# A streamed two-layer trunk on one core: state products interleaved with projections, earlier adaLN pieces, and a third fixed expert in the second unit

## The chip, the cores and the metric

The kernel runs on one core of one Trainium2 chip. The metric is the device time of one execution in microseconds (us), the median over several runs. A core has a matrix engine (TensorE, PE in the profile, with its weight loads as PEld), a vector engine (DVE), a scalar engine (ACT), GpSimd (POOL) and SyncE (SP), which here does little else than issue the transfers of the weights. Each engine works through its own queue of instructions in order and waits for others by semaphores.

## The reference

The input is one sequence of 256 tokens of 1024 numbers. It passes through two layers, each a mixer and a mixture of experts, with weights in float32. Cut to what matters:

```python
cond = jax.nn.silu(c)
for i in range(2):
    sh1, sc1, g1, sh2, sc2, g2 = jnp.split(cond @ ada_w[i] + ada_b[i], 6, axis=-1)
    h = modulate(rmsnorm(x, norm_mix_g[i]), sh1, sc1)
    mix = gla_mixer(...) if i == 0 else lru_mixer(...)
    x = x + g1[:, None] * mix
    h = modulate(rmsnorm(x, norm_ffn_g[i]), sh2, sc2)
    x = x + g2[:, None] * grouped_moe(h, router_w, router_bias, w_gate[i], w_up[i], w_down[i])
return rmsnorm(x, final_norm_g)

def grouped_moe(...):      # per token: sigmoid scores, the best of 4 groups, the best 2 of its 4 experts
    for e in range(16):
        he = silu(t @ w_gate[e]) * (t @ w_up[e])          # 1024 -> 512
        out = out + combine[:, e:e + 1] * (he @ w_down[e])
```

`gla_mixer` is gated linear attention in chunks of 64 tokens: projections q, k, v and g, a state per chunk and head (k transposed times v, decayed), the output q times the state, normalised and multiplied by silu(g). Each token goes to two experts, so 512 pairs of token and expert are spread over 16 experts as the router decides. Which expert gets how many is data, and the inputs are drawn once from a fixed seed.

## The kernel before

**The stream of weights.** All large weights pass through one ring of 17 tiles of 1 MB (`SLOTS`). `plan` writes down the order of the pieces as a text: `a20` is the two pieces of adaLN column block 2, half 0 (`A` those of layer 1), `i4` two pieces of the mixer's input projection, `I3` and `J3` its first and second half alone, `o` the four of the output projection, `u0` the pieces of MoE unit 0. `Stream.get` hands out the next tile and calls `ahead`, which has SP issue transfers up to `look` pieces further on. A piece can be issued when its ring tile is free and when it is `known`: a piece of an expert that is chosen by rank is known only when `route_order` has written the list of ranks, `order[l]`.

**adaLN on DVE.** `fill` takes one job of a list: it gets two `a` pieces and lets DVE multiply them into a row (`scalar_tensor_tensor`, L317). `settle` later has TensorE sum and turn these rows.

**Layer 0's mixer (`gla`).** `half_proj` forms k and v, then q is formed (L613), then the products of the states (L629) for both tiles of 128 tokens, which DVE copies and scans out of the PSUM banks (L637), then the projection of g by `g_part` through `tok_proj` (L529), and `o_part`, `gated`, `turn`. `out_route` does the output projection (L473) together with the router.

**The MoE.** Tokens are gathered by expert into units of 128 rows, four slots of 32. `UNITS` lists them: `("s", 0, 2)` is the fixed expert 0 with 2 slots, `("r", 1, 3)` the expert that stands at rank 1 among those that are not fixed, sorted by their count of tokens, with 3 slots. `NS` is the number of fixed experts. `route_order` sorts, `route_end` works out where each expert's rows stand and compares each count with the expert's slots times 32 (`ce`). If one is greater, `fl` is 1. Each unit uses 12 MB of weights or more: two pieces of each of gate, up and down for each expert in it. `up_proj` (L1030) runs for gate and up, `down_proj` (L1041) and `scatter` (L1060, L1061) follow.

**`overflow`.** Ahead of unit 5 (`len(UNITS) - 2`) every engine reads the flag and branches (L1067). Only if it is set, a loop runs over all 16 experts (L1079 on): for each it loads the six pieces one after the other into the tile `h` (L1082), multiplies all 256 tokens with them, and adds the result for the tokens whose rank in their expert lies beyond the slots.

The pieces of code on which these words rest:

```python
V.tensor_tensor(ovf, cnt, ce, op=OP.is_gt)           # route_end
V.tensor_reduce(fl, ovf, axis=AX.X, op=OP.max)
...
with tc.If(flag > 0):                                # overflow, L1067
    ...
    with tc.For_i(0, NE, 1) as e:                    # L1079
        def load(name, n, j, q):
            t = h.rearrange("p m n -> p (m n)")
            nc.sync.dma_start(t, I[name][l][ds(e, 1), q * n:(q + 1) * n, :]...)   # L1082
```

Of the kernel before, what the change touches and what calls it, by code (L numbers as in the profile page):

```python
# [10 lines left out]
OP = mybir.AluOpType  # L11
# [3 lines left out]
P = 128  # L15
D = 1024
S = 256
NM = S // P
# [8 lines left out]

UNITS = [
    [("s", 0, 2), ("s", 1, 2)],
    [("r", 0, 3), ("r", 8, 1)],  # L30
    [("r", 1, 3), ("r", 9, 1)],
    [("r", 2, 2), ("r", 3, 2)],
    [("r", 4, 2), ("r", 5, 2)],
    [("r", 6, 2), ("r", 7, 2)],
    [("r", 10, 1), ("r", 11, 1), ("r", 12, 1), ("r", 13, 1)],
]
NS = 2
ND = NE - NS
SLOTS = 17
HALVES = [slice(0, 512), slice(512, 1024)]  # L40
# [35 lines left out]
def trunk(ctx, tc, I, out):  # L76
# [10 lines left out]
    def bank():  # L87
        return pp.tile([P, 512], F32, name="ps")
# [134 lines left out]
    late = []  # L223
# [6 lines left out]
    def moe_piece(l, name, kind, i, s, last):  # L230
        src = I[name][l]
        n, j = (512, 4) if name != "moe_w_down" else (256, 2)
        last = last and name == "moe_w_down"

        def f(t):
            if kind == "s":
                assert not last
                a = src[i, s * n:(s + 1) * n, :].rearrange("(p j) n -> p (j n)", j=j)
            else:
                if (l, i) not in regs:  # L240
                    with tc.issue_after(mark["load"]):
                        regs[l, i] = nc.sync.value_load(order[l][0:1, i:i + 1], min_val=NS, max_val=NE - 1)
                a = src[ds(regs[l, i], 1)]
                if last:

                    late.append((t, a))
                    part(t, a, s)
                    if len(late) == 2 * len(UNITS[-1]):
                        for q in range(2, len(TAIL)):
                            for t, a in late[len(UNITS[-1]):]:  # L250
                                part(t, a, q)
                        late.clear()
                    return
                a = a[:, s * n:(s + 1) * n, :].rearrange("o (p j) n -> (o p) (j n)", j=j)
            b = nc.sync.dma_start(t, a)  # L255
            mark["load"] = b.ins
        f.known = lambda: kind == "s" or order[l] is not None
        return f

    def moe_pieces(l, unit):  # L260
        return [moe_piece(l, name, kind, i, s, unit is UNITS[-1]) for name in ("moe_w_gate", "moe_w_up", "moe_w_down")
                for s in range(2) for kind, i, n in unit]

# [2 lines left out]
    def plan(l, text):  # L266

        for n in text.split():
# [13 lines left out]
            else:  # L282
                stream.add("u", *moe_pieces(l, UNITS[int(n[1])]))

    plan(0, "a10 a00 I2 a11 I3 a01 I1 J2 J3 J1 i0 a20 a21 i4 a40 a41 i5 a30 a31 a50 a51 o A10 A11 A00 A01 "
            "u0 u1 u2 u3 u4 u5 u6")
    plan(1, "i2 i3 a20 r i0 a21 a40 i1 a41 a30 a31 o a50 a51 u0 u1 u2 u3 u4 u5 u6")

# [171 lines left out]
    def out_route(l, yT, gate, gs, rest=None, last=None):  # L460

        w = [stream.get("o").rearrange("p (j n) -> p j n", j=2) for _ in range(4)]
        stream.look = SLOTS - 2
        h, hT = new_h()
        R = route_begin()

        def part(m, hf, between={}):
            sl = slice(hf * 512, (hf + 1) * 512)
            ps = bank()
            for k in range(8):  # L470
                if k in between:
                    between[k]()
                T.matmul(ps, yT[:, k, m * P:(m + 1) * P], w[k // 2][:, k % 2, sl], start=k == 0, stop=k == 7)  # L473
            tmp = s2("tmp")
            V.tensor_mul(tmp, ps, gate[:, sl])
            b = V.tensor_add(x[:, m, sl], x[:, m, sl], tmp)
            mark["x"] = b.ins

        def first():
            turn_h(x, hT, 0, halves=[1])  # L480
            stats_of[0] = stats(0)
            scaled(h, 0, stats_of[0])

        late = len(jobs) > 2
        stats_of = [None, None]
        with tc.manual_schedule(engines={T.engine}):
            part(0, 0)
            part(0, 1, {3: lambda: turn_h(x, hT, 0, halves=[0])})
            if rest:
                rest()  # L490
            router(R, gs)
            part(1, 0, {2: lambda: settle(2), 4: first, 6: lambda: router_shift(R, gs[1], 0), 7: lambda: logits(R, hT, 0)})
            router_shift(R, gs[1], 1)
            scores(R, 0, stats_of[0])
            choose(R, 0)
            fill(2)
            part(1, 1, {3: lambda: turn_h(x, hT, 1, halves=[0]), 5: lambda: logits(R, hT, 1, halves=[0]),
                        7: lambda: route_count(R, 0)})
            stream.ahead(stream.at + SLOTS - 1)
            r = stats(1)  # L500
            if late:
                accs = mid("acc")
                fill_now(accs[:, 0:512])
            else:
                settle(1)
            turn_h(x, hT, 1, halves=[1])
            xg, oh = gather_begin(R)
            gather_tile(R, h, oh, 0, 0, [0])
            logits(R, hT, 1, halves=[1])
            scores(R, 1, r)  # L510
            scaled(h, 1, r)
            gather_tile(R, h, oh, 0, 0, [1, 2, 3])
            choose(R, 1)
            gather_tile(R, h, oh, 0, 1)
            route_count(R, 1)
            if late:
                fill_now(accs[:, 512:1024])
            else:
                settle(1)
            if last:  # L520
                last()
            gather_end(l, R, h, xg, gs)
        R["xg"] = xg
        return h, hT, R
# [7 lines left out]
    def get2():  # L532
        return [stream.get("i").rearrange("p (j n) -> p j n", j=4) for _ in range(2)]


    def gla(gs):
# [40 lines left out]
            T.matmul(ps[32 * q:32 * q + 32, 0:S], wa[:, k, :], hT[:, k, :], start=k < 4, stop=k >= 4)  # L577
        V.tensor_scalar(alr, ps[:, 0:S], e16, None, op0=OP.add)
        half_proj(0, 1)
        for m in range(NM):  # L580
            A.copy(v[:, m, 0:512], pst[0][m])

# [5 lines left out]
        for m in range(NM):  # L588
            A.activation(ed[:, m], ed[:, m], AF.Ln, bias=1.0)
            V.scalar_tensor_tensor(la[:, m], psz[m], 0.0, ed[:, m], op0=OP.min, op1=OP.subtract)  # L590
        half_proj(1, 1)
        for m in range(NM):
            A.copy(v[:, m, 512:1024], pst[1][m])
        half_proj(2, 1)
        psg = bank()
        for m in range(NM):
            ps = bank()
# [12 lines left out]
        for hd in range(4):  # L610
# [1 line left out]
            for k in range(8):  # L612
                T.matmul(ps[:, 0:S], w[k // 4][:, k % 4, hd * P:(hd + 1) * P], hT[:, k, :], start=k == 0, stop=k == 7)  # L613
            A.activation(qT[:, hd], ps[:, 0:S], AF.Copy, scale=128.0 ** -0.5)
        fill(2)
        k0.extend(lru_consts())


        Sb = [big("S").rearrange("p (c n) -> p c n", c=2) for _ in range(2)]
        St = [Sb[c // 2][:, c % 2].rearrange("p (h n) -> p h n", h=4) for c in range(4)]  # L620

        for m in range(NM):
            for h2 in range(2):
                pair = [bank(), bank()]
                for hh in range(2):
                    hd = 2 * h2 + hh
                    for c in range(2):
                        rows_of = slice(64 * c, 64 * c + 64)
                        T.matmul(pair[c][:, hh * 256:(hh + 1) * 256], kd[rows_of, m, hd * P:(hd + 1) * P],  # L629
                                 v[rows_of, m, hd * 256:(hd + 1) * 256], start=True, stop=True)  # L630
                for c in range(2):
                    k = 2 * m + c
                    for hh in range(2):
                        hd = 2 * h2 + hh
                        src = pair[c][:, hh * 256:(hh + 1) * 256]
                        if k == 0:
                            V.tensor_copy(St[k][:, hd], src)  # L637
                        else:
                            V.scalar_tensor_tensor(St[k][:, hd], St[k - 1][:, hd], gam[:, hd * 4 + k:hd * 4 + k + 1],
                                                   src, op0=OP.mult, op1=OP.add)  # L640
        sg = big("sg").rearrange("p (m n) -> p m n", m=2)

        def g_part(hf, m, w):
# [26 lines left out]
        def turn(m, hf):  # L670
# [4 lines left out]
            for b in range(2):  # L675
# [4 lines left out]
                else:  # L680
                    V.tensor_scalar(dst, src, ngT[:, b:b + 1], None, op0=OP.mult)

        w = get2()
        for m in range(NM):
            g_part(0, m, w)
        fill(2)
        os = [o_part(m) for m in range(NM)]
        for m in range(NM):
            gated(m, 0, *os[m])
        settle(2)  # L690
        w = get2()
        g_part(1, 0, w)
        gated(0, 1, *os[0])
# [2 lines left out]
            turn(m, 0)  # L696
        g_part(1, 1, w)
        gated(1, 1, *os[1])
        fill(4)
        settle(2)  # L700
        turn(0, 1)
        return oT[0], lambda: turn(1, 1)

# [289 lines left out]
    def moe(l, h, hT, R, gs, g2, done=None):  # L993
# [18 lines left out]
        def groups(unit):  # L1012
# [7 lines left out]
                at += n  # L1020
            return res

        def up_proj(unit, xg, t0):
            ps = bank()
            for s in range(2):
                w = [stream.get("u").rearrange("p (j n) -> p j n", j=4) for _ in unit]
                for j in range(4):
                    k = 4 * s + j
                    for i, p0, n in groups(unit):
                        T.matmul(ps[p0:p0 + n], xg[:, k, t0 + p0:t0 + p0 + n], w[i][:, j, :], start=k == 0, stop=k == 7)  # L1030
            return ps
# [217 lines left out]
```

## Time and profile before

| | us |
|---|---|
| median of three runs | 759.18 |
| the three runs | 758.07, 759.18, 760.01 |
| profiled execution | 757.96 |
| its span | 756.2 |
| TensorE busy | 699.6 (93%) |
| DVE busy | 340.4 (45%) |
| ACT busy | 131.4 (17%) |

The span is the time from the first to the last recorded instruction; 1.8 us of the execution lie around it. A share of busy time is a mean over stages with different limits, so a stage has to be looked at by itself. The granted clock is 1.00 where TensorE runs at its higher level and 0.50 where it runs at its lower one. Transfers moved 286.27 MB, a mean of 379 GB/s over the span. In the timeline a group of instructions has its start, its length, and in square brackets the idle time ahead of it with what ended it.

### The profile page before, as it was taken

How to read it: one execution, taken by the hardware profiler on the slowest of the kernel's cores; microseconds unless marked ns; L12 is line 12 of the kernel's file. 1: busy time of each engine (PE TensorE's matmuls, PEld its weight loads, DVE VectorE, ACT ScalarE, POOL GpSimd, SP SyncE). 2: the span in 40 equal slices, each digit the busy share in tenths (PEclk: the TensorE clock that was granted, in tenths of full speed). 3: DMA queues.
4: the chain of work that ended last, by engine and by line, in shares of the span. 5: the costliest groups of instructions: out<-in, count | busy, mean ns of one | idle time of the engine just before them, and what ended most of it. 6: DMA issues, size and time to landing. Idle time of an engine off the chain costs nothing. (4 is left out here: it accounts for less than half of the span.)

```text
span 756.2 us, 9538 instructions
## 1 busy us (share of the span) xinstructions
PE 699.6 (93%) x3559; PEld 342.8 (45%) x3559; DVE 340.4 (45%) x780; ACT 131.4 (17%) x257; POOL 27.4 (4%) x69
## 2 busy tenths in 40 slices
PE   4899899999999999999887999998999999999874
PEld 3345745454633533533226888655433433433212
DVE  3626983897413223231023589996523143140214
ACT  5006112122200000000013166123210010010002
POOL 5000001000000000000000014000000000000000
PEclk9999999999999999999999999999999999999998
DMA  9999999779999999999999999991999999999994
GB/s 304 384 386 387 386 396 386 269 318 384 423 370 422 421 421 420 423 409 422 411 363 379 381 367 350 406 377 59 423 421 419 419 421 421 421 420 410 422 373 150
DMA packets 80445, 286.27 MB, mean 379 GB/s; under 512 B 5991, under 2 KB 16280, under 8 KB 57866
## 3 DMA queue, kind: packets, MB, share of 16 engines
q1 hardware_dynamic: 78752, 284.71, 96.0%
q10 hardware_dynamic: 1258, 0.66, 0.3%
q8 instruction: 30, 0.49, 0.3%
q0 software_dynamic: 384, 0.23, 0.1%
q14 instruction: 21, 0.17, 0.1%
HBM read 284.54 MB, written 1.05 MB: 378 GB/s over the span
## 5 line engine op out<-in xcount | busy, mean ns | idle before, releaser
L1030 PE MATMUL ps<-w 128*32 128x512 f32 (+1 forms) x1280 | 204.1, 593 | 9.6 <-DMA w<-in_moe_w_up_dram 7.4
L1030 PEld LDWEIGHTS ps<-w 128*32 128x32 f32 (+1 forms) x1280 | 61.8, 121 | 148.7 <-issue 121.7
L1041 PE MATMUL ps<-w,s 128*32 128x512 f32 (+1 forms) x512 | 85.0, 594 | 2.7 <-ACT s L1160 2.7
L1147 DVE TENSOR_TENSOR s<-s,ps 128x512 f32<-128x512 f32 x14 | 9.6, 688 | 149.6 <-PE ps L1030 149.6
L1061 DVE TENSOR_TENSOR x<-x,ps 128x512 f32<-128x512 f32 (+1 forms) x60 | 39.1, 652 | 59.7 <-PE ps L1060 59.7
L317 DVE SCALAR_TENSOR_TENSOR acc<-w,cond,acc 128x512 f32<-128x512 f32 x84 | 64.8, 794 | 1.1
L473 PE MATMUL ps<-w 128*128 128x512 f32 x128 | 59.3, 599 | 0.0
L1060 PE MATMUL ps<-mid,s 128*128 128x512 f32 (+1 forms) x120 | 55.1, 581 | 2.9 <-DVE mid L1168 2.6
L740 PE MATMUL ps<-hT,w 128*128 128x256 f32 x256 | 55.7, 379 | 0.0
L1041 PEld LDWEIGHTS ps<-w,s 128*32 128x32 f32 (+1 forms) x512 | 25.6, 123 | 58.3 <-issue 50.9
L740 PEld LDWEIGHTS ps<-hT,w 128*128 128x128 f32 x256 | 48.7, 191 | 6.7 <-ACT hT L423 0.2
L1179 DVE TENSOR_TENSOR mid<-ps,gate 128x512 f32<-128x512 f32 x24 | 16.6, 692 | 64.7 <-PE ps L1041 64.7
L561 PE MATMUL ps<-w,hT 128*128 128x512 f32 x96 | 42.5, 596 | 1.8 <-DVE hT L425 1.0
L904 PE MATMUL ps<-onehot,h 128*128 128x256 f32 x192 | 42.4, 379 | 0.0
L317 DVE SCALAR_TENSOR_TENSOR gate<-w,cond,gate 128x512 f32<-128x512 f32 x56 | 40.9, 748 | 0.9
L1146 ACT ACTIVATE s<-ps 128x512 f32<-128x512 f32 x14 | 8.4, 597 | 183.6 <-PE ps L1030 183.6
L904 PEld LDWEIGHTS ps<-onehot,h 128*128 128x128 f32 x192 | 36.4, 190 | 7.0 <-issue 2.4
L1060 PEld LDWEIGHTS ps<-mid,s 128*128 128x128 f32 x120 | 20.5, 190 | 30.8 <-issue 20.1
L1160 ACT COPY s<-ps 128x512 f32<-128x512 f32 x14 | 8.2, 586 | 147.2 <-PE ps L1158 147.2
L529 PE MATMUL ps<-w,hT 128*128 128x512 f32 x64 | 29.6, 619 | 3.7 <-DVE w L637 3.7
L473 PEld LDWEIGHTS ps<-w 128*128 128x128 f32 x128 | 22.8, 191 | 20.7 <-issue 18.9
L561 PEld LDWEIGHTS ps<-w,hT 128*128 128x128 f32 x96 | 17.8, 190 | 23.9 <-issue 21.0
(261 smaller groups left out, 602.5 us busy)
## 6 DMA issues: line engine op xcount, KB each, us to landing
w<-in_moe_w_gate_dram SPq DMA_DIRECT2D x64, 1024.0 KB, 11.2
w<-in_moe_w_up_dram SPq DMA_DIRECT2D x64, 1024.0 KB, 15.7
w<-in_moe_w_down_dram SPq DMA_DIRECT2D x56, 1024.0 KB, 17.8
w<-in_ada_w_dram SPq DMA_DIRECT2D x48, 1024.0 KB, 13.5
w<-in_gla_w_in_dram SPq DMA_DIRECT2D x12, 1024.0 KB, 14.6
w<-in_moe_w_down_dram SPq DMA_DIRECT2D x16, 512.0 KB, 9.5
w<-in_lru_w_in_dram SPq DMA_DIRECT2D x8, 1024.0 KB, 12.5
w<-in_gla_w_out_dram SPq DMA_DIRECT2D x4, 1024.0 KB, 12.5
```

What stands on the lines that cost most here:

```text
L317: V.scalar_tensor_tensor(acc, w, cond[:, k:k + 1], acc, op0=OP.mult, op1=OP.add)
L473: T.matmul(ps, yT[:, k, m * P:(m + 1) * P], w[k // 2][:, k % 2, sl], start=k == 0, stop=k == 7)
L529: T.matmul(ps, hT[:, k, m * P:(m + 1) * P], w[k // 4][:, k % 4, :], start=k == 0, stop=k == 7)
L561: T.matmul(pst[i][m], hT[:, 4 * b + j, m * P:(m + 1) * P], w[:, j], start=b == 0 and j == 0, stop=b == 1 and j == 3)
L740: T.matmul(ps[:, 0:S], w[k // 4][:, k % 4, ct * P:(ct + 1) * P], hT[:, k, :], start=k == 0, stop=k == 7)
L904: T.matmul(ps[j // 2][:, j % 2 * 2 * P:(j % 2 + 1) * 2 * P], hv[:, b, j, :], oh, start=m == 0 and j % 2 == 0, stop=m == 1 and j % 2 == 1, ...
L1030: T.matmul(ps[p0:p0 + n], xg[:, k, t0 + p0:t0 + p0 + n], w[i][:, j, :], start=k == 0, stop=k == 7)
L1041: T.matmul(ps[hf][p0:p0 + n], aT[:, k, p0:p0 + n], w[i][:, j, hf * 512:(hf + 1) * 512], start=k == 0, stop=k == 3)
L1060: T.matmul(ps, wt[:, m * P:(m + 1) * P], y[:, sl], start=True, stop=True)
L1061: V.tensor_add(x[:, m, sl], x[:, m, sl], ps)
L1147: V.tensor_mul(act, act, pu)
L1179: V.tensor_mul(y[:, sl], py[hf], g2[:, sl])
```

## The change

Three things are altered.

First, the units of the MoE. `NS` is 3: expert 2 is fixed too and shares unit 1 with rank 1, which now has two slots instead of three. Rank 0 and rank 8 move to unit 2, and the last unit holds ranks 9 to 12. Unit 1's pieces come in another order, gate and up of expert 2 first, and `up_proj` takes its pieces by a list `held` to match.

Second, the order of layer 0's pieces: `a20`, `a21`, `a40`, `a41`, `a30` and others stand among the input projections, and `A10 A11` ahead of `o`. The calls of `fill` and `settle` follow: one `fill` behind each of three `half_proj`, and none within `out_route` of layer 0 (`late` is true there).

Third, `states(m)` is a function, called ahead of `g_part(0, m)` for each tile of tokens, where all states stood before all of the projection.

```diff
 UNITS = [
     [("s", 0, 2), ("s", 1, 2)],
+    [("s", 2, 2), ("r", 1, 2)],
     [("r", 0, 3), ("r", 8, 1)],
-    [("r", 1, 3), ("r", 9, 1)],
...
-    [("r", 10, 1), ("r", 11, 1), ("r", 12, 1), ("r", 13, 1)],
+    [("r", 9, 1), ("r", 10, 1), ("r", 11, 1), ("r", 12, 1)],
 ]
-NS = 2
+NS = 3
...
     def moe_pieces(l, unit):
+        if unit is UNITS[1]:
+
+            return [moe_piece(l, name, kind, i, s, False) for kind, i, n in unit for name in ("moe_w_gate", "moe_w_up")
+                    for s in range(2)] + [moe_piece(l, "moe_w_down", kind, i, s, False) for s in range(2) for kind, i, n in unit]
...
-    plan(0, "a10 a00 I2 a11 I3 a01 I1 J2 J3 J1 i0 a20 a21 i4 a40 a41 i5 a30 a31 a50 a51 o A10 A11 A00 A01 "
+    plan(0, "a10 a00 I2 a11 I3 a01 I1 J2 a20 J3 a21 J1 a40 i0 a41 a30 i4 a31 a50 a51 i5 A10 A11 o A00 A01 "
             "u0 u1 u2 u3 u4 u5 u6")
...
-        late = len(jobs) > 2
+        late = rest is not None
...
-            fill(2)
+            if not late:
+                fill(2)
...
         half_proj(0, 1)
+        fill()
...
         half_proj(1, 1)
+        fill()
...
         half_proj(2, 1)
+        fill()
...
-        fill(2)
+        fill()
+        settle(3)
+        fill()
         k0.extend(lru_consts())
...
         w = get2()
         for m in range(NM):
+            states(m)
             g_part(0, m, w)
-        fill(2)
+        settle(1)
+        with tc.issue_after(mark["states"]):
+            fill(3)
...
-        settle(2)
...
-        fill(4)
         settle(2)
+        fill(2)
         turn(0, 1)
...
+        held = []
+
         def up_proj(unit, xg, t0):
             ps = bank()
+            if unit is UNITS[1] and not held:
+                look, stream.look = stream.look, stream.look - 4
+                held.extend(stream.get("u") for _ in range(4))
+                stream.look = look
             for s in range(2):
-                w = [stream.get("u").rearrange("p (j n) -> p j n", j=4) for _ in unit]
+                w = [(held.pop(0) if held and i == 0 else stream.get("u")).rearrange("p (j n) -> p j n", j=4)
+                     for i in range(len(unit))]
```

On SP, in layer 0 from the output projection's pieces to the first piece of an expert that is chosen by rank (`TENSOR_LOAD r_ordi` reads the list of ranks), before:

```order
L211 DMA w<-in_gla_w_out_dram 128x2x1024 x4
L196 DMA w<-in_ada_w_dram 128x4x512 x8
L255 DMA w<-in_moe_w_gate_dram 128x2048 x4
L255 DMA w<-in_moe_w_up_dram 128x2048 x4
L255 DMA w<-in_moe_w_down_dram 128x2048 x4
L242 TENSOR_LOAD r_ordi
```

and now:

```order
L196 DMA w<-in_ada_w_dram 128x4x512 x4
L211 DMA w<-in_gla_w_out_dram 128x2x1024 x4
L196 DMA w<-in_ada_w_dram 128x4x512 x4
L255 DMA w<-in_moe_w_gate_dram 128x2048 x4
L255 DMA w<-in_moe_w_up_dram 128x2048 x4
L255 DMA w<-in_moe_w_down_dram 128x2048 x4
L255 DMA w<-in_moe_w_gate_dram 128x2048 x2
L255 DMA w<-in_moe_w_up_dram 128x2048 x2
L242 TENSOR_LOAD r_ordi
```

Four adaLN pieces moved ahead of the output projection, and four pieces of expert 2 (gate and up) now stand ahead of the list of ranks.

On TensorE, in layer 0 from the q projection (L613, now L621) to the second half of the g projection (L529, now L534); a product of the order is two passes in the trace. The states are L629 (now L681), `o_part` L655 (now L645). Before:

```order
L613 MATMUL ps<-hT,w 128x256 x32
L707 MATMUL ps<-ident,s_158 128x64
L629 MATMUL ps<-w,h 128x256 x16
L529 MATMUL ps<-w,hT 128x512 x16
L655 MATMUL ps<-w,mid 64x256 x16
```

and now:

```order
L621 MATMUL ps<-hT,w 128x256 x32
L353 MATMUL ps<-gate,one 128x512 x2
L357 MATMUL ps<-ident,acc 128x128 x4
L721 MATMUL ps<-ident,s_160 128x64
L681 MATMUL ps<-w,h 128x256 x8
L534 MATMUL ps<-w,hT 128x512 x8
L681 MATMUL ps<-w,h 128x256 x8
L534 MATMUL ps<-w,hT 128x512 x8
L357 MATMUL ps<-ident,acc 128x128 x4
L645 MATMUL ps<-w,mid 64x256 x16
```

The sixteen products of the states are split in two lots of eight with eight of the projection between them, and sums of adaLN rows stand ahead of them and behind.

## Rows read from the trace of the kernel before

**Rows 1.** The page, busy time, share of the span, instructions:
```profile
PE 699.6 (93%) x3559; PEld 342.8 (45%) x3559; DVE 340.4 (45%) x780; ACT 131.4 (17%) x257; POOL 27.4 (4%) x69
```

**Rows 2.** Windows around layer 1's routing; columns in the first line:
```profile
core 0: us, PE busy (x) PEld busy (x) DVE busy (x) ACT busy (x) POOL busy (x), PEclk, DMA share, GB/s
...
510.00:520.00 10.00, 8.74 (x41) 5.36 (x41) 5.79 (x29) 2.82 (x7) 0.55 (x1) 1.00 0.27 107
520.00:530.00 10.00, 8.62 (x51) 5.57 (x52) 7.29 (x38) 4.15 (x9) 0.00 (x0) 1.00 0.14 39
530.00:540.00 10.00, 10.00 (x50) 3.37 (x48) 5.98 (x30) 1.78 (x2) 0.00 (x0) 1.00 1.00 423
```

**Rows 3.** Timeline of TensorE: start, length, line, operation, [idle ahead <- releaser]:
```profile
73.37 14.00 PE L613 MATMUL ps<-hT,w 128*128 128x256 f32 x64
...
94.81 15.51 PE L529 MATMUL ps<-w,hT 128*128 128x512 f32 x32 [3.72 <-DVE w L637]
...
131.68 8.75 PE L473 MATMUL ps<-w 128*128 128x512 f32 x20
...
332.23 9.23 PE L1030 MATMUL ps<-w 128*64 128x512 f32 x42 [1.33 <-DVEq L1067]
...
481.04 9.61 PE L473 MATMUL ps<-w 128*128 128x512 f32 x22
```

**Rows 4.** Windows around the pause at 91 us, layer 0:
```profile
91.00:94.40 3.40, 0.09 (x2) 0.00 (x0) 2.95 (x19) 0.00 (x0) 0.00 (x0) 1.00 1.05 387
94.50:97.80 3.30, 2.99 (x4) 1.44 (x5) 3.30 (x10) 0.00 (x0) 0.00 (x0) 0.50 1.05 387
97.90:101.30 3.40, 3.40 (x9) 1.48 (x8) 3.37 (x8) 0.00 (x0) 0.00 (x0) 1.00 1.05 387
```

**Rows 5.** The instructions of one line, asked for the loop's load:
```profile
nothing on L1082; most used: ['L1030', 'L1041', 'L255', 'L740', 'L1052', 'L904', 'L473', 'L1060', 'L561', 'L317', 'L353', 'L766', 'L338', 'L529', 'L613', 'L830', 'L922', 'L1158', 'L433', 'L227', 'L196', 'L242', 'L1061', 'L818', 'L629']
```

**Rows 6.** The same view of the branch's line; durations in ns, minimum, median, maximum:
```profile
L1067 PEldq COMPARE_BRANCH  x2: 318/335/352, 328.9 to 674.0; - x2
```

**Rows 7.** DMA issues at 466, 160, 336 and 556 us; KB, us to landing:
```profile
w<-in_lru_w_out_dram SPq DMA_DIRECT2D x1, 1024.0 KB, 4.8
...
w<-in_moe_w_up_dram SPq DMA_DIRECT2D x1, 1024.0 KB, 4.9
...
w<-in_moe_w_gate_dram SPq DMA_DIRECT2D x1, 1024.0 KB, 5.9
...
w<-in_moe_w_gate_dram SPq DMA_DIRECT2D x1, 1024.0 KB, 7.7
```

**Rows 8.** The page's costliest groups: busy us, mean ns | idle before, releaser:
```profile
L1147 DVE TENSOR_TENSOR s<-s,ps 128x512 f32<-128x512 f32 x14 | 9.6, 688 | 149.6 <-PE ps L1030 149.6
L1061 DVE TENSOR_TENSOR x<-x,ps 128x512 f32<-128x512 f32 (+1 forms) x60 | 39.1, 652 | 59.7 <-PE ps L1060 59.7
L317 DVE SCALAR_TENSOR_TENSOR acc<-w,cond,acc 128x512 f32<-128x512 f32 x84 | 64.8, 794 | 1.1
...
L1146 ACT ACTIVATE s<-ps 128x512 f32<-128x512 f32 x14 | 8.4, 597 | 183.6 <-PE ps L1030 183.6
...
L1160 ACT COPY s<-ps 128x512 f32<-128x512 f32 x14 | 8.2, 586 | 147.2 <-PE ps L1158 147.2
```

**Rows 9.** Waits of SP's queue: us in total, times, longest us:
```profile
SPq L1067 <- SPq L1067: 18.6, 6, 6.3
```

**Rows 10.** Timeline of SP, layer 1: gate pieces of two units, four units apart:
```profile
555.74 4.34 SPq L255 DMA_DIRECT2D w<-in_moe_w_gate_dram  x4
...
669.21 17.06 SPq L255 DMA_DIRECT2D w<-in_moe_w_gate_dram  x8
```

**Rows 11.** DMA issues at 38.1 us (`i0`) and 107.0 us (`o`):
```profile
w<-in_gla_w_in_dram SPq DMA_DIRECT2D x1, 1024.0 KB, 15.0
...
w<-in_gla_w_out_dram SPq DMA_DIRECT2D x1, 1024.0 KB, 10.7
```

More of the change, by code (lines that the diff above doesn't have):

```diff
@@ L491, in out_route @@
             router(R, gs)
-            part(1, 0, {2: lambda: settle(2), 4: first, 6: lambda: router_shift(R, gs[1], 0), 7: lambda: logits(R, hT, 0)})
+            part(1, 0, {2: lambda: late or settle(2), 4: first, 6: lambda: router_shift(R, gs[1], 0), 7: lambda: logits(R, hT, 0)})
             router_shift(R, gs[1], 1)
@@ L620, in gla @@
         St = [Sb[c // 2][:, c % 2].rearrange("p (h n) -> p h n", h=4) for c in range(4)]
[L622 to L640, printed above, removed]
         sg = big("sg").rearrange("p (m n) -> p m n", m=2)
@@ L681, in turn, with states @@
                     V.tensor_scalar(dst, src, ngT[:, b:b + 1], None, op0=OP.mult)
+        def states(m):
+            for h2 in range(2):
+                pair = [bank(), bank()]
+                for hh in range(2):
+                    hd = 2 * h2 + hh
+                    for c in range(2):
+                        rows_of = slice(64 * c, 64 * c + 64)
+                        T.matmul(pair[c][:, hh * 256:(hh + 1) * 256], kd[rows_of, m, hd * P:(hd + 1) * P],
+                                 v[rows_of, m, hd * 256:(hd + 1) * 256], start=True, stop=True)
+                for c in range(2):
+                    k = 2 * m + c
+                    for hh in range(2):
+                        hd = 2 * h2 + hh
+                        src = pair[c][:, hh * 256:(hh + 1) * 256]
+                        if k == 0:
+                            b = V.tensor_copy(St[k][:, hd], src)
+                        else:
+                            b = V.scalar_tensor_tensor(St[k][:, hd], St[k - 1][:, hd], gam[:, hd * 4 + k:hd * 4 + k + 1],
+                                                   src, op0=OP.mult, op1=OP.add)
+            mark["states"] = b.ins
         w = get2()
         for m in range(NM):
+            states(m)
             g_part(0, m, w)
-        fill(2)
+        settle(1)
+        with tc.issue_after(mark["states"]):
+            fill(3)
         os = [o_part(m) for m in range(NM)]
```

## The prediction

> **What bounds the kernel now.** The profiled execution took 757.96 us: a span of 756.2 us and 1.8 us around it. I began with the page's busy times: TensorE works for 93% of the span [rows 1], so outside a few holes a change pays only where it fills one, or costs where it opens one. Then the windows. Where layer 1's routing is done, TensorE is 87% busy, DVE and ACT no more, while the transfers, 423 GB/s a moment later, fall to 107 and 39 GB/s [rows 2]: SP has no known piece left to fetch, and waits for the list of ranks. In layer 0 TensorE stands still for 3.72 us ahead of the gate projection, waiting for DVE [rows 3]; behind that pause its granted clock reads 0.50 (1.2 GHz, the lower of its two levels) for 3.3 us, then 1.00 again [rows 4]. Those are the two holes that the change aims at. Last I looked for the loop of `overflow()`. The kernel runs it only if an expert has more tokens than its slots hold. Its lines have no record, and the branch above it was passed twice, once for each layer [rows 5, 6]: here all experts fit, and the loop costs nothing but the branch.
>
> **The change, part by part. Slots of rank 1.** This decides. With a third fixed expert in unit 1, rank 1 keeps two slots (64 tokens) where it had three (96). Capacity matters only against the tokens that are routed, and the inputs are fixed, so I worked the reference's router over them. Layer 0 gives experts 0 to 15 these tokens: 19, 32, 31, 40, 49, 25, 75, 33, 6, 7, 2, 11, 44, 13, 46, 79. Experts 0 to 2 are now the fixed ones (at most 32 in 64). Rank 0 is expert 15 with 79 in 96. Rank 1 is expert 6 with 75 tokens, and its capacity is now 64. `route_end` compares with "greater", so layer 0's flag becomes 1. Before, 75 stood in 96. In layer 1 the two largest that are not fixed are 73 and 64: 64 against 64 is just not greater, and the loop stays out. So the loop runs in layer 0, ahead of unit 5, and it isn't a loop over the 11 tokens too many: it takes all 16 experts over all 256 tokens.
>
> **One turn of the loop.** No trace shows it, so I build it from its instructions. Six pieces of 1 MB go one after the other into one tile, `h`: each load must wait for the products that read the piece before it, and each product for its load, so they add up.
> - A load: 4.8 and 4.9 us where little else was under way, 5.9 us in a busier place [rows 7]. SP issues nothing else within the loop; I take 4.85, with 5.9 as the upper end.
> - Eight products of 128x128x512, of two passes each. `out_route` has the same shape: 22 passes in 9.61 us, 0.437 each [rows 3]; 16 take 7.0 us.
> - Two handoffs, load to TensorE and back: no row prices them. I put 0.1 us on each, the difference of the two quiet loads.
> - Clock. TensorE stands still for some 5 us at each load, longer than the 3.72 us after which it read 0.50. There it started 4 passes in 3.3 us, where the rate of 0.437 has 7.5 [rows 4]. So 3.5 passes are lost, 1.5 us, 1.6 with the edges. Lower end: nothing, if the clock holds. I take 1.6, since that is the nearest pause with the same product behind it.
> One piece: 4.85 + 7.0 + 0.2 + 1.6 = 13.65 us; six are 81.9. Between gate, up and down lie a silu, a product and a copy (597, 688, 586 ns [rows 8]) for two tiles of tokens and eight transposes: some 3.8 us on two engines that partly overlap, while `w_down`'s first piece takes 4.85 to land, so nothing. Without that cover they would cost up to 3.8 us a turn. At the end the last of four DVE pairs stands alone: 0.79 + 0.65 = 1.4 us [rows 8], and the engines meet before the next turn. For that, with the branch, a register for the expert and its address, I take 2 us: the branch alone kept TensorE for 1.33 us [rows 3] (lower end), SP waited 6.3 us at most there [rows 9] (upper end), and a branch takes only 0.3 us of PE's sequencer [rows 6], so nearer to the lower. A turn is 81.9 + 1.4 + 2.0 = 85.3 us, and 16 turns are 1365 us.
>
> On the load there is a rule that differs. The Trainium skill, "DMA: Bandwidth & Descriptors", section "Anatomy of one DMA — SWDGE (gpsimd) path", fits 2.0 us and bytes over 436 GB/s to one transfer, which gives an estimate of 4.4 us for 1 MB; by it the 96 loads would come to 43 us less. The trace's quiet loads on SP's queue took 4.8 and 4.9 us [rows 7], so I keep these.
>
> Entry and exit: the first load stands behind pieces in flight, and x must be turned again into `hT`; in return unit 5 finds its pieces landed when the loop is over. I put it at nothing, with 10 us either way, a third of a unit's 28.4 us (four units lie between the two issues at 555.74 and 669.21 us [rows 10]).
>
> **Third fixed expert, the rest of it.** Four more pieces can go before the ranks are known. At 423 GB/s [rows 2] they fill 4 x 2.48 = 9.9 us of the hole. But the unit after them is fetched into slots that TensorE frees, and there pieces already take 7.7 us to land instead of 4.85 [rows 7]: they queue some 2.8 us. That is all the lead the end can get back; I count 2.7 us gain in layer 1, between 0 and 9.9. Layer 0 keeps its transfers busy through routing, and I count nothing there.
>
> **States between projections.** `g_part(0, m)` stands behind `states(m)`, so TensorE has 16 passes to do while DVE empties the banks of the states. The pause of 3.72 us goes, and with it 1.6 us of low clock: 5.3 us, between 0 and 5.3. Next in line is the weight: `fill` moved forward puts adaLN pieces ahead of others.
>
> **adaLN pieces.** At 387 GB/s a piece takes 2.71 us [rows 4]. `i0` comes six pieces later: it was issued at 38.1 and landed 15.0 us later [rows 11], 53.1 + 16.3 = 69.4 us, and its products start at 73.4 [rows 3]. `o` comes four pieces later: issued at 107, landed after 10.7, 117.7 + 10.8 = 128.5, while its products began at 131.7 [rows 3, 11] and would now begin 5.3 us sooner, at 126.4. Its four pieces are used in turn, the last some 2.6 us after the first, so it is a tie: nothing, or up to 2 us of the 5.3 lost. DVE does the same work, earlier.
>
> **Sum.** 757.96 - 5.3 - 2.7 = 750, + 1365 = 2115 us. The median of the runs, 759.18, is 1.2 us above the profiled one, far below the errors of the sum.
>
> **The rivals.**
> B, the flag stays 0: the change does only what it says. It needs rank 1 of layer 0 at 64 tokens or fewer, where the count has 75. For it speaks only that the chip's router rounds otherwise; eleven of 256 tokens would have to change expert. Time: 750.0 us, faster.
> C, the low clock stays through the loop, since TensorE never works long between pauses. For it: after each pause 0.50 is read; against it: the clock came back after 3.3 us [rows 4], and a piece is longer than that. A pass then takes 0.87: 14.0 + 4.85 + 0.2 = 19.05, six are 114.3, + 3.4 = 117.7, x16 = 1883: 2633 us.
> D, layer 1 overflows as well: rank 1 has exactly 64, and one more token sets its flag. Against it: the choice would have to turn on rounding for a token. Time: 750 + 2 x 1365 = 3480 us.
> E, the clock doesn't fall: 12.0 x 6 + 1.4 + 2 = 75.4, x16 = 1206: 1956 us.
>
> **How the numbers follow.** Forecast 0.74, E 0.08, C 0.08, D 0.05, B 0.04, others 0.01. Low end: quiet loads, no clock loss, the shortest turn: (4.8 + 0.2 + 7.0) x 6 + 1.4 + 1.3 = 74.7, x16 = 1195: 1945 us. High end: loads of 5.9 and turns of 6.3: 14.7 x 6 + 1.4 + 6.3 = 95.9, x16 = 1534, with 10 for entry and exit 2294, 2300 rounded. B, C and D lie outside, 17 in 100. A difference of 0.3% is about what a measurement of this kernel can tell from no change; faster by that 0.04 (B), within it 0.01, slower 0.95.
>
> **What would show it.** Right: one stretch of some 1.36 ms ahead of layer 0's unit 5, with 96 loads of `h` from the three expert weights, TensorE idle for about 5 us ahead of each group of 16 passes, its clock at 0.50 at the start of each, transfers at about 74 GB/s (6.29 MB in 85.3 us); elsewhere no pause ahead of the gate projection, and 9.9 us less of a hole in layer 1. Wrong: no record on the loop's lines (B), two such stretches (D), passes of 0.87 us throughout (C), or loads that overlap the products.

## The result: 2119 us, the loop runs in layer 0

The changed kernel takes 2119.06 us, median of four runs (2117.30 to 2121.06), against 759.36 us before; the ratio is 2.791 (95% interval 2.786 to 2.796). The forecast was 2115 us. Its profiled execution has a span of 2115.3 us. From its page come the busy times, the slices (40 of 52.9 us each), and the products and loads of the loop, of which the kernel before has no record [rows 5]:

```profile
PE 1569.1 (74%) x5047; PEld 709.6 (34%) x5047; DVE 460.8 (22%) x971; ACT 172.1 (8%) x327; POOL 27.0 (1%) x71
...
PEclk9999998888888888888888888888888899999999
DMA  9998994221221221122122212221221299979998
GB/s 356 387 403 343 421 421 178 79 79 60 79 79 59 79 79 68 71 79 79 64 75 79 76 63 79 79 75 64 79 79 59 80 361 374 368 323 389 420 418 309
...
L1117 PE MATMUL ps<-h,hT 128*128 128x512 f32 x1024 | 569.3, 720 | 358.1 <-DMA h<-in_moe_w_gate_dram 203.0
...
L1139 PE MATMUL ps<-h,mid 128*128 128x512 f32 x512 | 282.0, 713 | 130.8 <-DMA h<-in_moe_w_down_dram 130.8
...
h<-in_moe_w_gate_dram SPq DMA_DIRECT2D x32, 1024.0 KB, 4.8
h<-in_moe_w_up_dram SPq DMA_DIRECT2D x32, 1024.0 KB, 4.8
h<-in_moe_w_down_dram SPq DMA_DIRECT2D x32, 1024.0 KB, 4.8
```

TensorE was 93% busy in [rows 1] and is 74% busy now. From slice 8 to slice 32 the transfers move 59 to 80 GB/s instead of some 400: that is one load of 1 MB at a time. The new groups carry 1536 passes, 16 experts x 6 pieces x 16 passes, and there are 96 loads into `h`, which land 4.8 us after their issue (median). The fit that the prediction weighed (the Trainium skill, "DMA: Bandwidth & Descriptors", section "Anatomy of one DMA — SWDGE (gpsimd) path", an estimate of 4.4 us) is given there for transfers that GpSimd issues; these loads on SP's queue took 0.4 us more. Over all 96, from the view of their line:

```profile
DMA to landing us min/median/max: 4.6/4.8/8.4
```

The 8.4 is the first one, which stands behind pieces of the stream.

Three windows go from layer 0's first MoE product to the end, split where `overflow` begins (326.2, x is turned into `hT` again) and at unit 5's first product (columns as in [rows 2]):

```profile
174.60:326.20 151.60, 150.92 (x757) 64.54 (x757) 49.16 (x116) 15.06 (x27) 0.00 (x0) 1.00 0.96 396
326.20:1696.00 1369.80, 872.63 (x1683) 364.37 (x1682) 122.00 (x193) 40.40 (x70) 0.00 (x0) 0.86 0.21 75
1696.00:2115.00 419.00, 386.31 (x1968) 192.27 (x1968) 173.75 (x375) 69.88 (x140) 13.31 (x6) 0.98 0.95 374
```

1369.8 us lie between, where [rows 3] have a pause of 1.33. One turn and the start of the next, then the start of the sixteenth, on TensorE's timeline:

```profile
336.65 8.93 PE L1117 MATMUL ps<-h,hT 128*128 128x512 f32 x16 [8.52 <-DMA h<-in_moe_w_gate_dram]
350.33 8.83 PE L1117 MATMUL ps<-h,hT 128*128 128x512 f32 x16 [4.75 <-DMA h<-in_moe_w_gate_dram]
363.99 8.83 PE L1117 MATMUL ps<-h,hT 128*128 128x512 f32 x16 [4.82 <-DMA h<-in_moe_w_up_dram]
377.63 8.83 PE L1117 MATMUL ps<-h,hT 128*128 128x512 f32 x16 [4.82 <-DMA h<-in_moe_w_up_dram]
386.30 0.63 PE L1128 MATMUL ps<-ident,mid 128*128 128x128 f32 x4
387.31 0.74 PE L1128 MATMUL ps<-ident,mid 128*128 128x128 f32 x4 [0.38 <-DVE mid L1124]
391.46 8.80 PE L1139 MATMUL ps<-h,mid 128*128 128x512 f32 x16 [3.40 <-DMA h<-in_moe_w_down_dram]
405.03 8.83 PE L1139 MATMUL ps<-h,mid 128*128 128x512 f32 x16 [4.76 <-DMA h<-in_moe_w_down_dram]
421.73 9.06 PE L1117 MATMUL ps<-h,hT 128*128 128x512 f32 x16 [7.87 <-DMA h<-in_moe_w_gate_dram]
...
1616.22 9.14 PE L1117 MATMUL ps<-h,hT 128*128 128x512 f32 x16 [7.83 <-DMA h<-in_moe_w_gate_dram]
```

Within gate, up and down the distance from one piece to the next is 13.57 to 13.68 us (13.83 where the tokens are turned), pause and products end to end, and the next turn begins 85.08 us after the first (421.73 - 336.65). Over 15 turns the mean is 85.30 us ((1616.22 - 336.65) / 15). The second pause and the products behind it, cut where the clock changes:

```profile
345.60:350.30 4.70, 0.00 (x0) 0.00 (x0) 0.00 (x0) 0.00 (x0) 0.00 (x0) 1.00 0.61 223
350.60:353.90 3.30, 3.30 (x5) 1.24 (x5) 0.00 (x0) 0.00 (x0) 0.00 (x0) 0.50 0.00 0
354.10:359.00 4.90, 4.90 (x12) 1.90 (x10) 0.00 (x0) 0.60 (x1) 0.00 (x0) 1.00 0.00 0
```

TensorE did nothing for 4.7 us; then it works at the lower level (0.50, 1.2 GHz) for 3.3 us and at the higher one behind that, as in [rows 4]. Outside the loop, the products of the states lie between those of the projections (timeline of TensorE, to be held against the 3.72 us of [rows 3]):

```profile
89.62 2.05 PE L681 MATMUL ps<-w,h 64*128 64x256 f32 x16
91.60 7.13 PE L534 MATMUL ps<-w,hT 128*128 128x512 f32 x16
98.66 2.79 PE L681 MATMUL ps<-w,h 64*128 64x256 f32 x16
101.38 7.13 PE L534 MATMUL ps<-w,hT 128*128 128x512 f32 x16
...
128.62 9.61 PE L477 MATMUL ps<-w 128*128 128x512 f32 x22
...
174.62 10.95 PE L1051 MATMUL ps<-w 128*64 128x512 f32 x50
```

There is no pause left, and the output projection (L477) starts 3.1 us before the 131.68 of [rows 3], with no wait for its pieces. Around layer 1's routing, which comes 1361 us later than in [rows 2] (the output projection ahead of it starts at 1842.20 instead of 481.04), the transfers now read 375, 160 and 233 GB/s:

```profile
1870.00:1880.00 10.00, 8.84 (x38) 5.14 (x36) 6.59 (x29) 2.52 (x6) 0.00 (x0) 1.00 0.92 375
1880.00:1890.00 10.00, 8.51 (x52) 6.29 (x54) 6.72 (x38) 3.56 (x6) 0.55 (x1) 1.00 0.38 160
1890.00:1900.00 10.00, 10.00 (x48) 3.30 (x46) 6.67 (x33) 2.69 (x4) 0.00 (x0) 1.00 0.59 233
```

The first two are more than the 107 and 39 of [rows 2], the third is less than its 423. These windows lie 1.2 us earlier in the routing than those of [rows 2], so they don't give the size of what was filled; e8, below, has them in the same place.

### The profile page after: what moved, and what is told of

The parts are those of the page before. It is cut to its first block, busy times and chain, and to the rows that moved or that the text cites. A ratio compares the mean times of both kernels' runs of the same rounds, so it can differ in the third digit from the quotient of the medians.

```text
span 2115.3 us, 14212 instructions
## 1 busy us (share of the span) xinstructions
PE 1569.1 (74%) x5047; PEld 709.6 (34%) x5047; DVE 460.8 (22%) x971; ACT 172.1 (8%) x327; POOL 27.0 (1%) x71
## 5 line engine op out<-in xcount | busy, mean ns | idle before, releaser
L1117 PE MATMUL ps<-h,hT 128*128 128x512 f32 x1024 | 569.3, 720 | 358.1 <-DMA h<-in_moe_w_gate_dram 203.0
L1117 PEld LDWEIGHTS ps<-h,hT 128*128 128x128 f32 x1024 | 229.9, 230 | 696.9 <-issue 424.6
L1139 PE MATMUL ps<-h,mid 128*128 128x512 f32 x512 | 282.0, 713 | 130.8 <-DMA h<-in_moe_w_down_dram 130.8
L1124 DVE TENSOR_TENSOR mid<-mid,ps 128x512 f32<-128x512 f32 x32 | 22.0, 688 | 868.3 <-PE ps L1117 868.3
L1139 PEld LDWEIGHTS ps<-h,mid 128*128 128x128 f32 x512 | 113.8, 228 | 288.9 <-issue 198.3
L1051 PE MATMUL ps<-w 128*64 128x512 f32 (+1 forms) x1152 | 201.5, 593 | 7.5 <-DMA w<-in_moe_w_up_dram 4.6
L1145 DVE SCALAR_TENSOR_TENSOR mid<-ps,o_cc,gate 128x512 f32<-128x512 f32 x64 | 48.0, 751 | 355.4 <-PE ps L1139 355.4
L1051 PEld LDWEIGHTS ps<-w 128*64 128x64 f32 (+1 forms) x1152 | 63.2, 125 | 142.4 <-issue 121.5
L1062 PE MATMUL ps<-w,s 128*64 128x512 f32 (+1 forms) x448 | 85.0, 595 | 2.7 <-ACT s L1181 2.7
L477 PE MATMUL ps<-w 128*128 128x512 f32 x128 | 59.1, 599 | 0.0
L1146 DVE TENSOR_TENSOR x<-x,mid 128x512 f32<-128x512 f32 x64 | 44.3, 692 | 2.2
L566 PE MATMUL ps<-w,hT 128*128 128x512 f32 x96 | 42.4, 595 | 1.6 <-DVE hT L429 1.0
```

The source lines that it names most:

```text
L566: T.matmul(pst[i][m], hT[:, 4 * b + j, m * P:(m + 1) * P], w[:, j], start=b == 0 and j == 0, stop=b == 1 and j == 3)
L1062: T.matmul(ps[hf][p0:p0 + n], aT[:, k, p0:p0 + n], w[i][:, j, hf * 512:(hf + 1) * 512], start=k == 0, stop=k == 3)
L1117: T.matmul(pm[m], hT[:, k, m * P:(m + 1) * P], w[:, j], start=k == 0, stop=k == 7)
L1139: T.matmul(py[m][hf], aTs[m][:, k], w[:, j, hf * 512:(hf + 1) * 512], start=k == 0, stop=k == 3)
L1145: V.scalar_tensor_tensor(tmp, py[m][hf], cc[:, m:m + 1], g2[:, sl], op0=OP.mult, op1=OP.mult)
```

## Experiments

The theory: rank 1's 75 tokens against 64 set the flag, and the loss is the 16 turns of the loop, each of six loads and six groups of products end to end with a low clock behind each load. The rivals: the loss comes from the new units as well; entry and exit of the loop weigh; products in the loop are slow in themselves; the loads are bound by their queue. All ratios are to the kernel before on the same chip.

| run | median us | ratio (95%) |
|---|---|---|
| the change | 2119.06 | 2.791 (2.786 to 2.796) |
| e1, no loop, no branch (leaves out rank 1's expert for eleven tokens) | 749.06 | 0.986 (0.985 to 0.988) |
| e2, one turn | 840.21 | 1.107 (1.104 to 1.109) |
| e3, before with rank 1 in two slots | 2126.30 | 2.802 (2.797 to 2.807) |
| e4, every count fits | 753.02 | 0.991 (0.990 to 0.993) |
| e12, the same again | 752.80 | 0.991 (0.990 to 0.993) |
| e9, every count fits, no branch | 750.33 | 0.988 (0.986 to 0.990) |
| e10, branch one unit later | 752.82 | 0.992 (0.990 to 0.993) |
| e7, states and adaLN alone | 755.63 | 0.994 (0.993 to 0.996) |
| e8, third fixed expert alone | 757.12 | 0.997 (0.996 to 0.998) |
| e5, spare products in the pauses | 1987.41 | 2.618 (2.613 to 2.622) |
| e6, two tiles for the loads | 1607.16 | 2.117 (2.113 to 2.120) |
| e11, 63 instead of 64 | 3487.70 | 4.595 (4.583 to 4.607) |

**What sets the flag.** The one number that the theory blames, changed in the kernel before:

```diff
-    [("r", 1, 3), ("r", 9, 1)],
+    [("r", 1, 2), ("r", 9, 2)],
```

> The kernel before with one number changed: rank 1 has two slots instead of three, and rank 9 takes the free one. Theory (75 tokens against 64 set the flag, whatever else is changed): 759 + 1368 = 2127 us. Rival (the flag comes from the units' new shape or the third fixed expert): 759 us.

It took 2126.3 us, 1367.6 more than the kernel before on its chip. The new units, the third expert and the order of pieces are not needed for the loss; the slot is. The other way round, the changed kernel with slots in which all counts fit:

```diff
-    [("s", 0, 2), ("s", 1, 2)],
-    [("s", 2, 2), ("r", 1, 2)],
+    [("s", 1, 2), ("s", 2, 2)],
+    [("s", 0, 1), ("r", 1, 3)],
```

> The changed kernel with expert 0 (19 and 27 tokens) in one slot of unit 1 and rank 1 in three slots, experts 1 and 2 in unit 0; every count fits, so the branch is passed and the loop doesn't run. Theory: the time of the run without the loop, about 751 us, with a branch more; the third fixed expert is kept. Rival (units of slots 1 and 3 cost TensorE more than 2 and 2): 755 us or more.

> The kernel in which every count fits once more, beside the two that differ from it by the branch, for one comparison on one chip: 753 us.

753.0 and 752.8 us: without the overflow the change is a gain of 0.9%, and this version beats both kernels. It rests on expert 0's counts as the change rested on rank 1's: by the router, worked over the inputs, 19 and 27 tokens of 32.

**The tie in layer 1.** In the changed kernel's table of capacities:

```diff
-            G.memset(c, float(n * 32))
+            G.memset(c, float(n * 32 - (kind == "r" and i == 1)))
```

> The changed kernel with rank 1's count compared with 63 instead of 64 (in layer 0 one token more goes to the loop; in layer 1 the rank-1 expert, if it has exactly 64 tokens as worked out from the inputs, overflows by one). Theory: layer 1 runs the loop too, 2119 + 1368 = 3487 us. Rival (the count in layer 1 on the chip is 63 or fewer): 2119 us. If it were 65, the changed kernel itself would have run the loop twice, which it did not.

3487.7 us. So layer 1's rank 1 holds exactly 64 tokens on the chip, and the change missed a second loop by one token. Its page shows the two stretches in the transfers:

```profile
GB/s 367 402 377 356 75 78 72 72 72 72 72 75 81 72 72 72 72 72 73 239 364 348 410 241 72 72 72 72 72 74 81 74 72 72 72 72 73 78 78 277
```

**What the loop is made of.** First with the call left out, then with one turn of sixteen:

```diff
                 pend = None
-                overflow()
```

> The changed kernel with the call of overflow() left out, so the eleven tokens beyond rank 1's slots in layer 0 lose that expert's part; nothing else differs. Theory (the loop is the whole loss): 2119 less 16 turns of 85.1 us and some 7 us of entry and exit, about 751 us, 0.989 of before. Rival (units in the new shape, or the pieces in the new order, cost time of their own): 759 us or more.

```diff
-                with tc.For_i(0, NE, 1) as e:
+                with tc.For_i(6, 7, 1) as e:
```

> The changed kernel with the loop over expert 6 alone, the only one with tokens beyond its slots; the sum over the other fifteen experts is zero. Theory (every turn costs the same and whole experts are paid for eleven tokens): 2119 less 15 turns of 85.1 us, 843 us. Rival (entering and leaving the loop is a large part of the 1368 us, the turns less): above 860 us.

749.06 and 840.21 us. (2119.06 - 840.21) / 15 = 85.26 us a turn, and 840.21 - 749.06 - 85.26 = 5.9 us for entering and leaving, the two branches included: the turns are the loss. (The three runs were on three chips, on which the kernel before took 758.72 to 759.49 us, so the 5.9 is good to about 1 us.) Expert 6's turn alone is what the data asks for, and 15 of 16 turns add zeros. The end of its timeline on TensorE, and unit 5's first products behind it:

```profile
407.98 8.83 PE L1139 MATMUL ps<-h,mid 128*128 128x512 f32 x16 [4.89 <-DMA h<-in_moe_w_down_dram]
419.00 6.23 PE L1051 MATMUL ps<-w 128*64 128x512 f32 x28 [2.20 <-DVE x L1146]
```

**The clock.** In the loop, spare products behind the groups, and TensorE's instructions held in the order of the text:

```diff
+                    spare = bank()
+                    def busy(n):
+                        for i in range(n):
+                            T.matmul(spare, ident, hT[:, 0:2, :].rearrange("p k t -> p (k t)"), start=True, stop=True)
...
+                            if name == "moe_w_gate" or q == 0:
+                                busy(5)
...
+                    busy(3)
                     py = [[bank() for _ in range(2)] for _ in range(NM)]
...
+                        if q == 0:
+                            busy(5)
```

> The changed kernel with 5 spare products of 128x128x512 (3 ahead of w_down's first piece) behind each group of products of the loop but the last of a turn, into a bank that nobody reads; they fit into the 4.8 us in which TensorE waits for a load. Theory (the 8.83 us of 16 passes are 7.0 us and the low clock behind the pause): 5 of 6 groups take 7.0 us with the clock at 1.00, a turn 9 us less: 1975 us. Rival (the products of the loop are slow in themselves, or the low clock has another cause): 2119 us or more.

1987.4 us: more work for TensorE, and 131.7 us less, 8.2 a turn where 9 were expected. The timeline of TensorE in one turn (L1124 are the products of the loop, L1112 the spare ones), and two windows, within that turn and around the next one's start:

```profile
415.75 9.59 PE L1124 MATMUL ps<-h,hT 128*128 128x512 f32 x16 [7.85 <-DMA h<-in_moe_w_gate_dram]
425.18 4.46 PE L1112 MATMUL ps<-hT,ident 128*128 128x512 f32 x10
430.19 7.13 PE L1124 MATMUL ps<-h,hT 128*128 128x512 f32 x16 [0.56 <-DMA h<-in_moe_w_gate_dram]
...
493.19 10.12 PE L1124 MATMUL ps<-h,hT 128*128 128x512 f32 x16 [7.83 <-DMA h<-in_moe_w_gate_dram]
```

```profile
429.00:486.00 57.00, 52.94 (x126) 22.66 (x124) 6.30 (x9) 2.37 (x4) 0.00 (x0) 1.00 0.21 77
486.00:503.00 17.00, 9.80 (x16) 4.23 (x17) 1.02 (x3) 0.00 (x0) 0.00 (x0) 0.70 0.16 62
```

The groups behind a pause of 0.5 to 0.8 us take 7.1 us at 1.00 throughout; the one group that still has the long pause ahead of it takes 9.6 or 10.1, more than the 9.06 of the change, which is part of why 8.2 us came and not 9. So 8.83 is 7.1 us of products and 1.7 of low clock, and the low clock goes with the pause.

**The shared tile.**

```diff
-SLOTS = 17
+SLOTS = 16
...
+    h2 = cst.tile([P, 2048], F32, name="h2")
...
+                        loads[0] += 1
-                        t = h.rearrange("p m n -> p (m n)")
+                        t = h.rearrange("p m n -> p (m n)") if loads[0] % 2 else h2
```

> The changed kernel with the loop's loads alternating between h and a second tile, for which the ring has 16 tiles instead of 17. Theory (a turn is six loads and six groups of products end to end, since they share one tile): loads lie beside the products, and a turn has one load of 4.85, six groups of 7.0, 3.5 us of silu and turning that nothing hides any more, 3.1 at its end and 1.8 of low clock, 55 us: 750 + 884 = 1634 us, some us more for the smaller ring. Rival (the loads are bound by their queue or the memory and not by the shared tile): 2000 us or more.

1607.2 us, 27 below what was expected, 1.7 us a turn: mostly since silu and turning leave 1.4 us between the products of up and those of `w_down` in the rows below, where 3.5 were put. On TensorE all four groups of gate and up stand in one row, and SP's first loads of two turns are 53.9 us apart:

```profile
392.91 30.70 PE L1120 MATMUL ps<-h,hT 128*128 128x512 f32 x64 [7.87 <-DMA h<-in_moe_w_gate_dram]
...
425.04 13.90 PE L1142 MATMUL ps<-h,mid 128*128 128x512 f32 x32
```

```profile
387.95 0.88 SPq L1106 DMA_DIRECT2D h<-in_moe_w_gate_dram  x2
...
441.83 0.87 SPq L1106 DMA_DIRECT2D h<-in_moe_w_gate_dram  x2
```

The loads were neither slow nor bound by the queue; they waited for their tile. What the smaller ring costs by itself was not measured.

**The rest of the change.** Its parts alone, each on top of the kernel before: e7 has the change's order of layer 0 with `NS = 2` and the units of before; e8 has `NS = 3`, the units of e4, `held` and the new order of unit 1's pieces, with layer 0 as before.

> States between projections and the earlier adaLN pieces alone, on the units of before. By the prediction 5.3 us less than before, by the trace of the change 4.5 us less (layer 0's first MoE product came at 174.6 us, not 179.1): 754.5 us. Rival (the gain is eaten later, since layer 0's transfers set the pace of the units): 759 us.

> The third fixed expert alone, in units in which every count fits (expert 0 in one slot and rank 1 in three in unit 1), the order of layer 0 as before. By the prediction 2.7 us less than before, bounds 0 and 9.9: 756.5 us. If the four pieces bring the whole hole back, 749.5; if nothing, 759.

755.63 and 757.12 us: 3.9 and 2.4 less than before (by the intervals of the ratios 3.4 to 5.4 and 1.5 to 3.3). Together 6.2, and e4 and e12 with both have 6.5 and 6.6 less, so the two gains add up. The windows of e8 around layer 1's routing, to be held against [rows 2]; the last line is the kernel before in the window that [rows 2] don't have:

```profile
510.00:520.00 10.00, 8.74 (x42) 5.36 (x41) 5.90 (x29) 2.80 (x7) 0.55 (x1) 1.00 0.99 405
520.00:530.00 10.00, 8.61 (x51) 5.70 (x52) 7.19 (x38) 4.23 (x9) 0.00 (x0) 1.00 0.28 116
530.00:540.00 10.00, 10.00 (x50) 3.30 (x46) 5.80 (x30) 1.72 (x2) 0.00 (x0) 1.00 0.72 283
...
550.00:560.00 10.00, 9.32 (x52) 3.63 (x55) 3.76 (x9) 1.05 (x2) 0.00 (x0) 1.00 0.64 248
```

```profile
550.00:560.00 10.00, 9.32 (x53) 3.63 (x55) 3.76 (x9) 1.05 (x2) 0.00 (x0) 1.00 1.01 421
```

In the first two windows e8 moves (405 - 107 + 116 - 39) x 10 us, 3.75 MB, more than the kernel before, 8.9 us of transfers. In the two others it moves (423 - 283 + 421 - 248) x 10 us, 3.13 MB, less. In between both read 424. So most of the hole was moved and not filled: over 510 to 560 us 0.62 MB are left, 1.5 us of transfers, and 2.4 us come out at the end. On SP the next unit's first gate piece is issued at 555.68 us in e8 and at 555.74 in the kernel before [rows 10]: it can't go before its ring tile is free.

**The branch.** e1 lies 4 us below e4. Two runs ask whether the branch or the units make it: e9 is e4 without the call, and e10 is

```diff
-            if u == len(UNITS) - 2:
+            if u == len(UNITS) - 1:
```

> The kernel in which every count fits (expert 0 in one slot, rank 1 in three) without the call of overflow(), so without the branch ahead of unit 5 in either layer; on these inputs the output is the same. What it tells apart: that kernel took 753.0 us, the changed kernel without the call 749.1. If the two branches make the 4 us (PE 1.3 us idle at each, SP's queue up to 7 us), this run takes 749 us; if units of slots 3 and 1 do, 753 us.

> The kernel in which every count fits, with the branch ahead of unit 6 instead of unit 5. If what the branch costs is SP's wait at it, while transfers for later units are due, it costs less where SP has most of the last unit's pieces issued: 751 us. If the cost is TensorE's pause at the branch, it stays: 753 us. If SP's wait holds back the last unit's 24 pieces, more: 755 us.

750.33 us without the branch, 752.82 one unit later, 752.80 where it was, all on one chip. Two branches cost about 2.5 us, the same in either place, which speaks against SP's wait for transfers that are due. TensorE's timeline in e12 shows the longer of its two pauses at the branch, which together are 2.2 us:

```profile
328.81 5.37 PE L1051 MATMUL ps<-w 128*64 128x512 f32 x24 [1.33 <-DVEq L1088]
```

The remaining 1.3 us between e9 and e1 may be the units of three slots and one; the two ran on different chips, the intervals of their ratios overlap, and it stays open.

## Why the prediction was right, step by step

**The counts.** Layer 0's flag, layer 1's tie and the place ahead of unit 5 came out as worked out from the inputs (e3, e11). Rivals B and D fall.

**A piece.** Forecast 4.85 + 0.2 + 7.0 + 1.6 = 13.65 us, measured 13.57 to 13.68 in the first turn. The mechanism was right, but that the sum is so close is in part luck: three terms were off and made up for each other. Load and handoffs together are the pause of 4.8 us: the 0.2 for handoffs aren't seen, since the load lands after 4.8 and the products start at once. The clock costs 1.7 us (8.83 against e5's 7.13), not 1.6, and the products 7.13, not 7.0. Rival C falls: by the page's busy times a group of 16 passes takes 8.87 us on the mean of all 96 ((569.3 + 282.0) / 96), not 14.0, and in the group cut above the clock is back after 3.3 us. Rival E falls by the same rows: without a loss to the clock a group takes the 7.13 us of e5.

**The end of a turn.** Forecast 1.4 + 2.0. From the last product's end at 413.86 to the next load's issue at 416.77 there are 2.9 us. DVE's last pair, on its timeline:

```profile
413.90 0.75 DVE L1145 SCALAR_TENSOR_TENSOR mid<-ps,o_cc,gate 128x512 f32<-128x512 f32 x1 [0.24 <-PE ps L1139]
414.68 0.69 DVE L1146 TENSOR_TENSOR x<-x,mid 128x512 f32<-128x512 f32 x1
416.75 0.17 DVE L1108 COPY o_cc<-o_co 128x2 f32 x1 [1.38 <-PEq L1100]
```

The pair ends 1.5 us behind the products, and 1.4 us pass until the engines have met and the branch is taken: the turn of the loop was over-sized by 0.6 us. The first group of a turn, which takes 9.06 us behind its longer pause, and the 13.83 us where the tokens are turned give some of that back. Silu and turning hide under `w_down`'s load, as forecast: the pauses of 3.40 and 0.38 us around them add up to less than one load.

**Entry and exit.** Put at nothing, within 10 us; 5.9 us by e2, and 2.5 of that is the branch, which was in the kernel before as well, so 3.4.

**The rest.** Forecast 8.0 us of gain, measured 6.5 (e4, e12) in units of three slots and one. In the change's own units an estimate is 7.9: e1's 749.06 is 10.4 below the kernel before on its chip, and 2.5 of that is the branches. The states and the adaLN pieces were sized at 5.3 and gave 3.9 in time and 4.5 in the trace (layer 0's first MoE product at 174.6 us instead of 179.1). Two rows of the kernel before, the states and that product:

```profile
87.32 3.77 PE L629 MATMUL ps<-w,h 64*128 64x256 f32 x32
...
179.15 6.23 PE L1030 MATMUL ps<-w 128*64 128x512 f32 x28
```

The pause of 3.72 and its low clock went whole. At the output projection the lead is only 3.1 us, since the prediction left out two things. The states in two lots take 2.05 + 2.79 us where they took 3.77. And 1.1 us of sums of adaLN rows (L353 of the kernel before, now L357) came out of `out_route` and stand ahead of it; with their old place empty, the lead has grown to 4.5 at the first MoE product. The tie at `o` cost nothing: TensorE came to it at 128.62 us, later than the forecast 126.4, and didn't wait. The third expert was sized at 2.7 and gave 2.4: what the pieces fetched early gain is given back for the most part within 50 us (e8's windows), since the units behind them wait for free slots, as the prediction had it.

In sum, 749.06 (e1) + 16 x 85.26 + 5.9 = 2119.1 us. This is no test, since 85.26 and 5.9 were worked out from the same three times; the trace's 85.30 us a turn is one, and so is e11, whose second loop cost 1368.6 us (3487.70 - 2119.06) where the first, both branches included, is 1370.1 (16 x 85.26 + 5.9). The forecast is 4.1 us short: 3.4 of it is entry and exit, 1.4 is that the sum starts from the profiled execution (757.96) and not from the median (759.36), and the turns give back 0.8 (1364.2 for 1365).

## What to carry to other kernels

A slow path that no trace shows is still part of the kernel's time: before a capacity is cut, work the data against it, and price the path from its instructions by rows of the same shape. Loads that share one tile with the products that read them add up instead of overlapping; here each of them left TensorE idle for 4.8 us and cost 1.7 us of low clock behind that, and a second tile (with one tile less in the ring) was worth 512 us of 1368. Fetching early helps little where the units behind wait for free tiles: here 3.13 of 3.75 MB brought forward were given back within 50 us. When a change bundles edits, time each alone: here one slot hid a gain of 0.9%.

## What the runs showed of the hardware

Spare work on TensorE made the kernel faster: 23 more products a turn took 8.2 us off it, since a group of 16 passes then took 7.13 us instead of 8.83.

The pause of 7.8 us between turns cost differently from kernel to kernel: the group behind it took 9.02 to 9.29 us in turns 2 to 16 of the change (pauses of 7.67 to 7.94 us) and 9.59 and 10.12 in two turns of e5 (pauses of 7.85 and 7.83). What sets the difference these runs don't tell.
